# Moving one step of a polynomial exp from VectorE to GpSimd in an attention kernel, with a new order of cells and casts

The kernel runs on one core of a Trainium2 chip. The metric is device time in microseconds (us): the median of the runs of one kernel, each run being the time of the core from launch to finish. The kernel before takes 397.42 us (397.2 to 397.73). The device time is about 1.8 us above the span that the profile shows, from the first to the last instruction.

## The reference

Grouped-query attention: 8 batches, 8 query heads that share 2 K/V heads, sequence 1024, head size 64, float32 in and out.

```python
q: (8, 8, 1024, 64)   k, v: (8, 2, 1024, 64)          # times 0.1
for g in range(n_kv_heads):                            # 4 query heads per K/V head
    scores = scale * np.matmul(q_group, k_group.transpose(0, 1, 3, 2))
    attn = np.exp(scores - scores.max(axis=-1, keepdims=True))
    attn = attn / (attn.sum(axis=-1, keepdims=True) + 1e-08)
    output[:, group] = np.matmul(attn, v_group)
```

## The kernel before

The work is cut into 128 **jobs** (batch, head, one of two sets of 512 queries), each of 8 **cells** (128 keys by 512 queries). TensorE makes the scores of a cell into PSUM. A cell then takes one of two ways. ScalarE takes two cells at a time with its exp function ("A" cells, in the PSUM tiles `aps`). VectorE takes single cells ("D" cells, in `dps`): it empties PSUM into integers that are already the bits of a rough bfloat16 exp, and then improves a group of cells with a curve in four steps, which I call AND, linear step, product and add.

```python
def exps(n, cells):                       # ScalarE, two cells
    nc.scalar.activation(out=pt[:, 0:m], in_=psum.pop(("A", n))[:, 0:m], func=AF.Exp, scale=scale)

def exp_bits(cell, n, g, slot):           # VectorE, one cell: empties PSUM
    nc.vector.tensor_scalar(out=groups[g][:, slot], in0=psum.pop(cell),
        scalar1=bits_scale, scalar2=bits_bias, op0=ALU.mult, op1=ALU.add)

def exp_curve(g, m, step):                # a group of GROUP = 4 cells
    if step == 0:    nc.vector.tensor_scalar(out=z, in0=pd, scalar1=0x7F, scalar2=None,
                                             op0=ALU.bitwise_and)          # AND
    elif step == 1:  nc.vector.tensor_scalar(out=y, in0=temps[g][0], scalar1=CURVE_A / 128.0,
                         scalar2=CURVE_B, op0=ALU.mult, op1=ALU.add)       # linear step
    elif step == 2:  nc.vector.tensor_tensor(out=y, in0=z, in1=y, op=ALU.mult)     # product
    else:            nc.vector.tensor_tensor(out=pd, in0=pd, in1=y, op=ALU.add)    # add
```

TensorE multiplies every finished cell with V (plus a column of ones for the sum), and VectorE normalises a job with a reciprocal and a multiplication.

K and q reach their transposed form through DRAM. GpSimd issues a **cast** (float32 to bfloat16 into scratch `scr_q`, `scr_k`, `scr_v`); once scores have begun, each cast also waits for the last score before it in the plan, which paces the casts. SyncE issues two **transposes** for each (`qT`, `kT`), and GpSimd issues four **placements** of `kT` into `kset`.

```python
def cast(key, src):           # GpSimd
    dma = nc.gpsimd.dma_start(out=scr..., in_=src...)
def transpose(key, dst, n):   # SyncE
    nc.sync.dma_start_transpose(out=dst[:, rows], in_=src[rows, :])
def place_k(b, g, side, parity):   # GpSimd
    nc.gpsimd.dma_start(out=ksets[b % 2][...], in_=kT[(b, g)][...])
```

Who does what when is fixed at build time. A small simulation (`make_plan`) gives each operation a planned time from fixed costs. Loads are hung in at planned distances before the first use of what they bring (`th`), and everything is issued in the order of these times. Each engine then works its own queue from front to back.

```python
for op in plan:
    at(op[0], run[op[1]], *op[2:])
...
    at(th - 28.0, cast, ("q", b, h), q[b, h])
    at(th - 17.0 + n, transpose_q, b, h, n)
    ...
    at(th - 27.0 + n, transpose_k, b, g, n)
    at(th - 20.0, place_k, b, g, side, parity)
```

The softmax here doesn't subtract the row's maximum and nothing guards it: scores larger than these inputs give would overflow.

Of the kernel before, what the change touches and what calls it, by code (L numbers as in the profile page):

```python
# [13 lines left out]

GROUP = 4


def make_plan(nj, nkc):
# [5 lines left out]

    QK, PV, EXP, P1, NORM = 0.214, 0.143, 0.925, 0.605, 0.57
    CHAIN = (0.73, 0.73, 1.26, 1.26)
    FROM_PE, FROM_ACT, FROM_DVE = 0.28, 0.18, 0.12
    LIVE_A, LIVE_D, PENDING, ONLY_A = 26, 6, 8, 14
    INF = 1e9
    n = nj * nkc  # L30
    ops = []
    pe = act = dve = 0.0
    a_free, bank, obank_free = [0.0, 0.0], [0.0, 0.0], [0.0, 0.0]
    nxt = 0
    open_jobs, next_job, rem, obank = [], 0, {}, {}
    open_a = None
# [4 lines left out]
    a_id = d_id = -1  # L41

    def first_free(slots):
        return min(range(len(slots)), key=lambda s: slots[s])

    while normed < nj:
        best = None
        if nxt < n:
            ta = td = INF
            if open_a is not None:  # L50
                ta = max(pe, open_a["t"])
            elif live["A"] < LIVE_A:
                ta = max(pe, min(a_free))
            if pending < PENDING and nxt < n - ONLY_A and (cur or live["D"] < LIVE_D):
                td = max(pe, min(bank))
            t, to_d = (ta, 0) if ta <= td else (td, 1)
            if t < INF:
                best = min(best or (INF,), (t, 1 + to_d, "qk", to_d))
        for i, s in enumerate(open_jobs):
            for c in rem[s]:  # L60
                at = max(pe, ready.get(s * nkc + c, INF))
                if at < INF:
                    best = min(best or (INF,), (at, 3 + i, "pv", (s, c)))
        if len(open_jobs) < 2 and next_job < nj:
            at = max(pe, min(obank_free), min(ready.get(next_job * nkc + c, INF) for c in range(nkc)))
            if at < INF:
                best = min(best or (INF,), (at, 3 + len(open_jobs), "open", next_job))
        for q, p, kind in ((normq, 0, "norm"), (p1q, 1, "p1"), (chainq, 2, "chain")):
            if q:
                best = min(best or (INF,), (max(dve, q[0][0]), p, kind, 0))  # L70
        if cur and nxt >= n - ONLY_A and not p1q:
            best = min(best or (INF,), (dve, 9, "flush", 0))
        t, _, kind, arg = best
        if kind == "qk":
            cell = nxt
            nxt += 1
            pe = t + QK
            if not arg:
                if open_a is None:
                    slot = first_free(a_free)  # L80
                    a_id += 1
                    live["A"] += 1
                    open_a = {"slot": slot, "t": a_free[slot], "cells": []}
                    a_free[slot] = INF
                o = open_a
                ops.append((t, "qk", cell, "A", a_id, o["slot"], len(o["cells"])))
                o["cells"].append(cell)
                home[cell] = ("A", a_id)
                if len(o["cells"]) == 2 or nxt >= n:
                    act = max(act, pe + FROM_PE)  # L90
                    ops.append((act, "exp", a_id, tuple(o["cells"])))
                    act += EXP * len(o["cells"]) / 2
                    a_free[o["slot"]] = act + FROM_ACT
                    uses[("A", a_id)] = len(o["cells"])
                    for x in o["cells"]:
                        ready[x] = act + FROM_ACT
                    open_a = None
            else:
                k = first_free(bank)
                bank[k] = INF  # L100
                pending += 1
                ops.append((t, "qk", cell, "D", k, 0, 0))
                p1q.append((pe + FROM_PE, cell, k))
# [44 lines left out]
        else:  # L148
            _, g, cells, step = chainq.pop(0)
            ops.append((t, "chain", g, len(cells), step))  # L150
            dve = t + CHAIN[step] * len(cells) / GROUP
            if step + 1 < len(CHAIN):
                chainq.insert(0, (dve, g, cells, step + 1))
            else:
                pending -= len(cells)
                uses[("D", g)] = len(cells)
                for x in cells:
                    ready[x] = dve + FROM_DVE
# [4 lines left out]
def kernel(  # L163
# [7 lines left out]
    nc = tc.nc  # L171
# [18 lines left out]
    E1 = D + 1  # L190
    PIECE = 256
    scale = 1.0 / math.sqrt(D)
    bits_scale = 128.0 * scale * math.log2(math.e)
# [13 lines left out]
    first_pool = ctx.enter_context(tc.tile_pool(name="firstp", bufs=1))  # L207
    qT_pool = ctx.enter_context(tc.tile_pool(name="qTpool", bufs=8))
    kT_pool = ctx.enter_context(tc.tile_pool(name="kTpool", bufs=4))
    pa_pool = ctx.enter_context(tc.tile_pool(name="papool", bufs=26))  # L210
    pd_pool = ctx.enter_context(tc.tile_pool(name="pdpool", bufs=6))
    tmp_pool = ctx.enter_context(tc.tile_pool(name="tmppool", bufs=2))
# [67 lines left out]
    def place_v(b, g):  # L280
        for two in range(2):
# [5 lines left out]
            )  # L287

    def first_loads():

        staged = []
        for eng, src in ((nc.sync, k[0, 0]), (nc.scalar, q[0, 0])):
            f = first_pool.tile([128, NHC, 2, D], FP32, name=f"f{len(staged)}")
            eng.dma_start(
                out=f, in_=src.rearrange("(c p two) d -> p c two d", p=128, two=2)
            )
            staged.append(f)
        vf = first_pool.tile([128, NHC, 2, D], FP32, name="vf")
        nc.sync.dma_start(
            out=vf, in_=v[0, 0].rearrange("(c p two) d -> p c two d", p=128, two=2)  # L300
        )
        cast(("q", 0, 1), q[0, 1])
        for two in range(2):
# [3 lines left out]
            )  # L307
        for side in range(2):
            nc.gpsimd.memset(ksets[1][(1 - side) * D : (2 - side) * D, :, side, :], 0.0)  # L309
        fk, fq = staged  # L310

        hk = first_pool.tile([128, NHC, 3, D], BF16, name="hk")
        nc.vector.tensor_copy(out=hk[:, :, 0:2, :], in_=fk)  # L313
        nc.vector.tensor_copy(out=hk[:, :, 2, :], in_=fk[:, :, 0, :])
        hq = first_pool.tile([128, NHC, 2 * D], BF16, name="hq")
        nc.scalar.copy(out=hq, in_=fq.rearrange("p c two d -> p c (two d)"))
        tk = dbanks[0].tile([128, 2, HALF], BF16, name="dps0")
        tq = dbanks[1].tile([128, HALF], BF16, name="dps1")
        for w in range(2):
            for c in range(NHC):  # L320
                nc.tensor.transpose(  # L321
# [3 lines left out]
                )  # L325
        for c in range(NHC):
            nc.tensor.transpose(tq[:, c * 128 : (c + 1) * 128], hq[:, c, :], ident)
        qT[(0, 0)] = qT_pool.tile([128, HALF], BF16, name="qT")
        lo, hi = slice(0, D), slice(D, 2 * D)
        nc.vector.tensor_copy(out=ksets[0][lo, 0, 0, 0:HALF], in_=tk[lo, 0, :])  # L330
        nc.scalar.copy(out=qT[(0, 0)], in_=tq)
        nc.vector.tensor_copy(out=ksets[0][lo, 0, 0, HALF:S], in_=tk[lo, 1, :])
        nc.vector.tensor_copy(out=ksets[0][hi, 0, 1, 0:HALF], in_=tk[hi, 1, :])
        nc.vector.tensor_copy(out=ksets[0][hi, 0, 1, HALF:S], in_=tk[hi, 0, :])

# [45 lines left out]
    def exp_curve(g, m, step):  # L381
# [7 lines left out]
        elif step == 1:  # L389
            y = tmp_pool.tile([128, GROUP, QBS], FP16, name="y")[:, 0:m]  # L390
            temps[g].append(y)
            nc.vector.tensor_scalar(  # L392
                out=y,
# [55 lines left out]
    for op in plan:  # L449
        if op[1] == "qk":  # L450
            first_use.setdefault(op[2] // NKC, op[0])
        at(op[0], run[op[1]], *op[2:])
    for b in range(B):
        for h in range(H):
            if b == 0 and h == 0:
                continue
            th = first_use[(b * H + h) * 2]
            if (b, h) != (0, 1):
                at(th - 28.0, cast, ("q", b, h), q[b, h])
            for n in range(HALF // PIECE):  # L460
                at(th - 17.0 + n, transpose_q, b, h, n)
            if h % HPG == 0:
                g = h // HPG
                at(th - 38.0, cast, ("k", b, g), k[b, g])
                at(th - 33.0, cast, ("v", b, g), v[b, g])
                for n in range(HALF // PIECE):
                    at(th - 27.0 + n, transpose_k, b, g, n)
                for side in range(2):
                    for parity in range(2):
                        at(th - 20.0, place_k, b, g, side, parity)  # L470
                at(th - 15.0, place_v, b, g)
# [34 lines left out]
```

## Time and profile before

The span is 395.6 us. Times in a timeline are counted from the start of the span. The prediction divides the span into what precedes the first exp, the exps, and what follows the last; it shows the busy table, the costliest groups and the timelines.

The view of the transfers in the first 16 us gives a queue with its packets, megabytes and share of the 16 DMA engines, and a group of issues with the median us from issue to landing (the last figure).

```profile
q0 software_dynamic: 192, 0.84, 31.9%
...
qT<-scr_q SPq DMA_TRANSPOSE x4, 3.1
```

In the head of the kernel before, ScalarE is busy for 11.46 of 11.80 us, the DMA engines are half used, and the transposes of q land 3.1 us after their issue. The software queue is the one with GpSimd's casts.

### The profile page before, as it was taken

Reading aid. Unit: us, or ns where it says so; the run is one execution under the profiler, and the core shown is the slowest. Engines: PE = TensorE matmul, PEld = TensorE weight load, DVE = VectorE, ACT = ScalarE, POOL = GpSimd, SP = SyncE. Lnnn points to the kernel's source line nnn. Section 1 sums busy time; section 2 is a strip of 40 time slices with the busy share of each in tenths; the row PEclk is TensorE's granted clock in tenths of the full one; section 3 lists DMA queues with packets and bytes.
Section 4 is the critical chain, followed back from the end, with each engine's and each line's share of the span. In section 5 each row is a group of like instructions: output and inputs, shape, how many; then the busy total and the mean of one; then the engine's idle time right before and its main releaser. Section 6 shows DMA issues by size and latency. Waiting matters only on the chain.

```text
span 395.6 us, 12683 instructions
## 1 busy us (share of the span) xinstructions
PE 365.7 (92%) x5043; PEld 233.0 (59%) x5132; DVE 375.8 (95%) x664; ACT 381.5 (96%) x415; POOL 86.6 (22%) x165
## 2 busy tenths in 40 slices
PE   4899999999999999999999999999999999999986
PEld 2455566565656556655656565565655666565655
DVE  4999999999999999999999999999999999999995
ACT  4999999999999999999999999999999999999992
POOL 5340303132041313113131040312214131120000
PEclk9999999999999999999999999999999999999999
DMA  4665866749676786847758686785965867574314
GB/s 106 106 125 111 163 107 127 128 86 160 103 139 130 132 143 101 142 90 145 115 103 141 111 141 112 118 143 98 155 109 115 149 132 121 99 130 99 68 28 94
DMA packets 134890, 46.72 MB, mean 118 GB/s; under 512 B 130848, under 2 KB 132384, under 8 KB 133344
## 3 DMA queue, kind: packets, MB, share of 16 engines
q1 hardware_dynamic: 129408, 29.52, 38.3%
q0 software_dynamic: 4896, 16.13, 27.0%
q8 instruction: 40, 0.66, 0.8%
q10 hardware_dynamic: 528, 0.26, 0.2%
q14 instruction: 18, 0.15, 0.2%
HBM read 27.13 MB, written 28.97 MB: 142 GB/s over the span
## 4 chain that ended last, share of the span: by engine, by line
ACT 67%; DVE 11%; PE 10%; issue 6%; DMA 3%; POOL 1%; SPq 0%
ACT pa L362 67%; PE ops L414 5%; PE aps L351 5%; DVE pd L371 3%; DVE y L402 2%; DVE pd L406 2%; DVE ost L429 1%; DMA vf<-in_v_dram 1%; PE dps L351 1%; DVE y L392 1%; DMA qT<-scr_q 1%; POOL kset L309 1%; DVE z L386 1%; DVE rec L427 1%; DMA scr_q<-in_q_dram 1%
## 5 line engine op out<-in xcount | busy, mean ns | idle before, releaser
L362 ACT ACTIVATE pa<-aps 128x1024 bf16<-128x1024 f32 x412 | 379.0, 1064 | 2.1 <-PE aps L351 1.3
L351 PE MATMUL aps<-qT,kset 128*128 128x512 bf16 x735 | 226.2, 379 | 15.5 <-ACT pa L362 13.6
L414 PEld LDWEIGHTS <-pa 128*128 128x128 bf16 x3296 | 134.5, 97 | 57.6 <-DVE ost L429 0.8
L414 PE MATMUL ops<-vset,pa 128*128 128x65 bf16 x3296 | 143.9, 193 | 3.4
L371 DVE TENSOR_SCALAR pd<-dps 128x512 uint16<-128x512 f32 x200 | 129.8, 682 | 2.2 <-PE dps L351 2.2
L351 PEld LDWEIGHTS <-kset 128*128 128x128 bf16 x1024 | 85.3, 97 | 66.3 <-issue 30.9
L248 POOL DMA_DIRECT2D scr_q<-in_q_dram x63 | 34.0, 540 | 173.4 <-PE aps L351 150.6
L351 PE MATMUL dps<-qT,kset 128*128 128x512 bf16 x200 | 64.5, 380 | 1.0
L406 DVE TENSOR_TENSOR pd<-pd,y 128x2048 uint16<-128x2048 uint16 x50 | 61.2, 1225 | 1.7
L402 DVE TENSOR_TENSOR y<-z,y 128x2048 f16<-128x2048 uint16 x50 | 61.2, 1225 | 1.7
L429 DVE TENSOR_TENSOR ost<-ops,rec 128x256 f32<-128x256 f32 x128 | 54.3, 425 | 4.4
L414 PEld LDWEIGHTS <-pd 128*128 128x128 bf16 x800 | 38.5, 97 | 29.8 <-DVE pd L406 7.9
L268 POOL DMA_DIRECT2D kset<-kT x60 | 32.2, 545 | 76.7 <-DMA kT<-scr_k 68.7
L414 PE MATMUL ops<-vset,pd 128*128 128x65 bf16 x800 | 45.3, 194 | 1.2
L392 DVE TENSOR_SCALAR y<-z 128x2048 f16<-128x2048 uint16 x50 | 34.3, 687 | 0.6
L386 DVE TENSOR_SCALAR z<-pd 128x2048 uint16<-128x2048 uint16 x50 | 34.2, 684 | 0.0
L427 DVE RECIPROCAL rec<-ops 128x4 f32<-128x4 f32 x128 | 22.6, 176 | 2.4 <-PE ops L414 1.9
L248 POOL DMA_DIRECT2D scr_v<-in_v_dram x15 | 7.6, 505 | 8.2 <-PE aps L351 7.1
L248 POOL DMA_DIRECT2D scr_k<-in_k_dram x15 | 8.1, 542 | 4.7 <-PE aps L351 4.3
L321 PE MATMUL dps<-ident,hk 128*128 128x128 bf16 x8 | 1.0, 311 | 5.0 <-DVE hk L313 5.0
L321 PEld LDWEIGHTS <-hk 128*128 128x128 bf16 x8 | 0.8, 141 | 5.0 <-DVE hk L313 5.0
L309 POOL MEMSET kset<- 64x2048 bf16 x2 | 3.6, 1798 | 0.1
(20 smaller groups left out, 9.7 us busy)
## 6 DMA issues: line engine op xcount, KB each, us to landing
out_dram<-ost SPq DMA_DIRECT2D x128, 128.0 KB, 3.2
scr_q<-in_q_dram POOLq DMA_DIRECT2D x63, 128.0 KB, 3.5
kset<-kT POOLq DMA_DIRECT2D x60, 64.0 KB, 2.7
qT<-scr_q SPq DMA_TRANSPOSE x126, 3.6
scr_k<-in_k_dram POOLq DMA_DIRECT2D x15, 128.0 KB, 4.2
scr_v<-in_v_dram POOLq DMA_DIRECT2D x15, 128.0 KB, 3.9
vset<-scr_v SPq DMA_DIRECT2D x30, 64.0 KB, 3.8
kT<-scr_k SPq DMA_TRANSPOSE x30, 3.4
```

The lines of the kernel that those rows point to most:

```text
L248: dma = nc.gpsimd.dma_start(out=scr.rearrange("(p f) -> p f", f=1024), in_=src.rearrange("(p s) d -> p (s d)", s=1024 // D),)
L268: nc.gpsimd.dma_start(out=ksets[b % 2][side * D : (side + 1) * D, g, side, parity * HALF : (parity + 1) * HALF], in_=kT[(b, g)][parity * D ...
L351: last_score[0] = nc.tensor.matmul(dst, lhsT=ksets[b % 2][:, h // HPG, side, c * 128 : (c + 1) * 128], rhs=qT[(b, h)], start=True, stop=Tr ...
L362: nc.scalar.activation(out=pt[:, 0:m], in_=psum.pop(("A", n))[:, 0:m], func=AF.Exp, scale=scale)
L371: nc.vector.tensor_scalar(out=groups[g][:, slot], in0=psum.pop(cell), scalar1=bits_scale, scalar2=bits_bias, op0=ALU.mult, op1=ALU.add,)
L386: nc.vector.tensor_scalar(out=z, in0=pd, scalar1=0x7F, scalar2=None, op0=ALU.bitwise_and)
L392: nc.vector.tensor_scalar(out=y, in0=temps[g][0], scalar1=CURVE_A / 128.0, scalar2=CURVE_B, op0=ALU.mult, op1=ALU.add,)
L402: nc.vector.tensor_tensor(out=y, in0=z, in1=y, op=ALU.mult)
L406: nc.vector.tensor_tensor(out=pd, in0=pd, in1=y, op=ALU.add)
L414: nc.tensor.matmul(ops_of[s][:, qs, :], lhsT=p_of[cell][:, qs * 128 : (qs + 1) * 128], rhs=vsets[b % 2][:, h // HPG, c, :], start=opens an ...
L427: nc.vector.reciprocal(out=rec, in_=o[:, :, D])
L429: nc.vector.tensor_tensor(out=ost, in0=o[:, :, 0:D], in1=rec.unsqueeze(2).to_broadcast([128, NQS, D]), op=ALU.mult,)
```

## The change

The intent is to relieve VectorE, so that it can take more cells from ScalarE. The linear step goes to GpSimd and runs there while VectorE empties PSUM. Groups grow from 4 to 8 cells. VectorE's cells come from jobs up to six further on (`LEAD`, growing by one every three jobs, `RAMP`), so that little is left at the end. Because those jobs come earlier, and because the planned distances before first use grow (for q in the first batch from 28 to 40), casts are issued sooner. The first loads come in halves, and 28 small matmuls warm TensorE.

```diff
-GROUP = 4
+GROUP = 8
+POOL_STEP = 1
...
+    LIVE_A, LIVE_D, PENDING, PER_JOB, LEAD, RAMP, AHEAD, FIRST_PV = 28, 5, 16, 2, 6, 3, 0.08, 2.0
...
+        lead = min(LEAD, job_a // RAMP)
+        job_d = max(job_d, job_a + lead)
+        while job_d < nj and (taken[job_d] >= PER_JOB or not todo[job_d]):
+            job_d += 1
...
-    qT_pool = ctx.enter_context(tc.tile_pool(name="qTpool", bufs=8))
+    qT_pool = ctx.enter_context(tc.tile_pool(name="qTpool", bufs=10))
...
-            nc.vector.tensor_scalar(
+            nc.gpsimd.tensor_scalar(
                 out=y,
                 in0=temps[g][0],
...
+    for side in range(2):
+        at(20.0 + 3.0 * side, blank_k, side)        # two memsets of the second K set, on GpSimd
...
-                at(th - 28.0, cast, ("q", b, h), q[b, h])
+                at(th - (34.0 if b else 40.0), cast, ("q", b, h), q[b, h])
-                at(th - 17.0 + n, transpose_q, b, h, n)
+                at(th - (21.0 if b else 17.0) + n, transpose_q, b, h, n)
...
-                at(th - 38.0, cast, ("k", b, g), k[b, g])
-                at(th - 33.0, cast, ("v", b, g), v[b, g])
+                at(th - 46.0, cast, ("k", b, g), k[b, g])
+                at(th - 42.0, cast, ("v", b, g), v[b, g])
-                    at(th - 27.0 + n, transpose_k, b, g, n)
+                    at(th - (31.0 if b else 19.0) + n, transpose_k, b, g, n)
-                        at(th - 20.0, place_k, b, g, side, parity)
+                        at(th - (15.0 if b else 8.0), place_k, b, g, side, parity)
```

Cut: the rest of the plan's new costs, the sizes of two other pools (`pa` 26 to 28, `pd` 6 to 5), and the first loads in halves.

## The prediction

> **What bounds the kernel now.** I read the page first: its busy table and its costliest groups.
>
> ```profile
> PE 365.7 (92%) x5043; PEld 233.0 (59%) x5132; DVE 375.8 (95%) x664; ACT 381.5 (96%) x415; POOL 86.6 (22%) x165
> L362 ACT ACTIVATE pa<-aps 128x1024 bf16<-128x1024 f32 x412 | 379.0, 1064 | 2.1 <-PE aps L351 1.3
> L371 DVE TENSOR_SCALAR pd<-dps 128x512 uint16<-128x512 f32 x200 | 129.8, 682 | 2.2 <-PE dps L351 2.2
> L406 DVE TENSOR_TENSOR pd<-pd,y 128x2048 uint16<-128x2048 uint16 x50 | 61.2, 1225 | 1.7
> L402 DVE TENSOR_TENSOR y<-z,y 128x2048 f16<-128x2048 uint16 x50 | 61.2, 1225 | 1.7
> L392 DVE TENSOR_SCALAR y<-z 128x2048 f16<-128x2048 uint16 x50 | 34.3, 687 | 0.6
> L386 DVE TENSOR_SCALAR z<-pd 128x2048 uint16<-128x2048 uint16 x50 | 34.2, 684 | 0.0
> ```
>
> ScalarE makes 412 exps of two cells each in 379.0 us, so 0.920 us apiece, and waits only 2.1 us before them. It is the bound. VectorE, which makes the other 200 of the 1024 cells, is as full: the two share the cells in proportion to speed. So the span has three parts: what precedes the first exp, the exps, and what follows the last. The timeline of ScalarE gives the first and third edges.
>
> ```profile
> 6.48 0.58 ACT L331 COPY qT<-dps 128x512 bf16<-128x512 bf16 x1 [0.93 <-PE dps L327]
> 8.16 6.04 ACT L362 ACTIVATE pa<-aps 128x1024 bf16<-128x1024 f32 x6 [1.10 <-PE aps L351]
> ...
> 384.37 3.84 ACT L362 ACTIVATE pa<-aps 128x1024 bf16<-128x1024 f32 x4
> ```
>
> First exp at 8.16, last one done at 388.21: 380.05 us between. The other 395.6 - 388.21 = 7.4 us are a tail in which TensorE works off products (the chain of waits ends in 3.14 us of them), VectorE normalises and the last output lands. The device time, 397.4, is 1.8 above the span.
>
> Last I read GpSimd's timeline and SyncE's, because the change puts arithmetic into GpSimd's queue, which until now holds almost only transfers.
>
> ```profile
> 10.37 0.52 POOL L248 DMA_DIRECT2D scr_q<-in_q_dram  x1
> ...
> 22.12 2.29 POOL L268 DMA_DIRECT2D kset<-kT  x4 [8.64 <-DMA kT<-scr_k]
> 24.40 0.52 POOL L248 DMA_DIRECT2D scr_q<-in_q_dram  x1
> ```
> ```profile
> 6.17 9.48 SPq L260 DMA_TRANSPOSE qT<-scr_q  x4
> 15.69 2.99 SPq L260 DMA_TRANSPOSE kT<-scr_k  x2
> ```
>
> GpSimd stands still for 8.64 us before it can issue the four placements of the second K group, since the transposes that make kT are issued by SyncE at 15.69 and land at 22.1. The cast behind them waits too, although it needs none of it: the queue is in order. Today this costs nothing. The reader should keep it in mind.
>
> **What the Trainium skill says.** "VectorE: DVE Perf Modes", section "The perf-mode tier table (the rule you actually need)", gives 693 ns for a 2048-element 16-bit tensor_scalar and 1224 ns for tensor_tensor. The trace agrees (684 to 687, and 1225). "SBUF — State Buffer", section "Who interferes with whom", says that a Vector instruction in a 2-port mode, or with two SBUF inputs against a GpSimd read, excludes GpSimd from a shared port, while one with at most one SBUF input outside those modes doesn't. No GpSimd arithmetic runs beside VectorE in the steady part of this trace, so nothing here tests it. "GPSIMD Engine Reference", section "4.1 Engine selection", calls one-input elementwise work on GpSimd roughly line-rate; section "3.1 Elementwise — side-by-side cycle accounting" has 1.03 cycles per element for light bodies. The trace's nearest rows are GpSimd's memset, 1798 ns for 2048 elements (0.88 ns each), and its casts, two of 256 elements in 0.74 us; both fit.
>
> **The change part by part.** Counts are from the instruction order of both builds.
> 1. Cells. ScalarE gets 406 exps instead of 412: 6 x 0.920 = 5.5 us less. The exps then need 406 x 0.920 = 373.5 us.
> 2. VectorE. The linear step leaves it, and groups have 8 cells. 212 emptyings at a pitch of 0.60 (two take 1.28 in the timeline) = 127; 128 normalisations at 0.55 = 70; 26 ANDs of 4096, estimated 684 + 2048/4/0.96 = 1217 ns, = 32; 52 tensor_tensors, estimated 1225 + 2048/2/0.96 = 2292 ns, = 119; one group of four adds 3. Sum 351 instead of about 391 at the same pitches (120 + 70 + 50 x 4.0). So VectorE gets some 30 us of slack, but the longest thing that holds it grows from 1.2 to 2.3 us.
> 3. GpSimd. 26 linear steps of 4096. Estimate from the memset's rate: 4096 x 0.88 + 0.2 = 3.8 us; with the skill's 1.03 cycles, 3.7. In every group the order puts only emptyings and normalisations of VectorE between the AND and the product: mostly 3 or 4 with 2 normalisations (about 3.5 us) or 6 with 3 (about 5.3 us). They read PSUM, so by the skill they aren't locked out, and the step is about hidden. Leftover waits: 1 us, a guess.
> 4. Head. K and q come in halves, TensorE is warmed by 28 small matmuls. The second half lands about when the whole did; TensorE saves 0.43 of the first two score matmuls' 0.86, but the warm-up itself may last till 5.5 to 6.0 (28 x 0.11 to 0.13 from 2.4) and hold up the transposes. I take the first exp at 7.5, 0.7 sooner.
> 5. Tail. VectorE's cells lie six jobs ahead, so at the end few products are left: two cells behind the last exp (0.2 + 0.3), then normalisation 0.9 and 3.1 us as now from the last ost to the end: 4.5 instead of 7.4, 2.9 less.
> 6. Casts sooner. Two memsets leave GpSimd's queue (3.65 us), and the casts start at about 7.1 instead of 10.37.
>
> Without a new wait: 7.5 + 373.5 + 1 + 4.5 = 386.5, plus 1.8 = 388.3. That would be 2.3% faster.
>
> **The new wait.** In the new order GpSimd's queue has the four kset placements of the second K group right in front of the first linear step. In SyncE's queue the transposes come as q1, q2, q3 (two each), then K's two. A transpose takes SyncE about 1.2 us. With q2's cast landing near 10 and q3's near 12.4, K's go out at 15 to 17 and land 4 to 4.6 later: at about 20.8. Four issues of 0.55 follow, so the first linear step starts at S = 23.1 and ends at 26.9. Its AND is done near 14.5.
> VectorE's queue has six emptyings after the AND and then the product that needs that step; the next two emptyings stand behind it. TensorE's queue has, behind the two D scores of those two emptyings, three more pairs for ScalarE, then D scores that need their banks. So the D score can't start before S + 3.85 + 2.3 + 0.6 + 0.1, and the second one, the next pair and the exp follow at S + 8.25 = 31.4. ScalarE has by then 18 exps: 7.5 + 18 x 0.92 = 24.1, with 0.7 more for q1's transpose, which lands at 11.3 where the order wants it near 10.5. It is then starved for about 31.4 - 24.8 = 6.6 us, and since it's the bound the loss is final. With K landing 2 us sooner or later the loss is 4.6 or 8.6.
> Sum: 386.5 + 0.7 + 6.6 = 393.8, plus 1.8 = 395.6. I lean a little to the lower side, as DMA times in the head are the shakiest of these: **394.8 us**, 0.7% faster.
>
> **The rivals.**
> A: the change works as it is meant to, K's transposes land early enough or fewer cells hang on the first group. Time 388 to 390. For it: every transfer starts earlier; the part after the head is sound. Against it: the in-order queue, shown by the 8.64 us wait above, and the position of the linear step behind it.
> B: the linear step on GpSimd is slow, or is held by port exclusion or transfers in its queue, in every group. Each us beyond about 3.8 stalls VectorE in some half of 27 groups, then TensorE's D scores. At 6 us per step: about 14 x 2.2 + 12 x 0.7 = 39 us less a part hidden in ScalarE's one exp of stock, so 405 to 430. Against it: memset and cast rates in this trace, and no Vector instruction with a second SBUF input inside the interval.
> C: nothing is stalled in the head, but 2.3 us tensor_tensors block both PSUM banks and starve ScalarE a little in each group, 26 x 0.2 = 5 us: 393. Against it: VectorE has slack, and D scores stand where the order expects a free bank.
>
> **Range and chances.** Main line 392 to 397 with about 70%, A 13%, C with or on top of the main line some 10%, B 7%. That gives 390 to 398.5 for 8 in 10. Two per cent faster means under 389.5: only A does it, 0.13. Two per cent slower is over 405.4: B, 0.06. Same: 0.81.
>
> **What would show it.** Right: ScalarE's exps 406 at about 0.92 mean pitch; a gap of 4 to 9 us in them between 23 and 33 us, with y's first instruction on GpSimd starting right behind four kset issues near 23 and the first product on VectorE waiting for POOL; hardly any gap after 40 us; first exp near 7.5; last exp to end near 4.5; GpSimd's linear step near 3.8 us; VectorE busy some 340 to 355 us. Wrong: kT landing before 16 us, or ScalarE without a gap in the head (A); a linear step over 5 us, or many waits of VectorE on POOL all along (B); many short waits of ScalarE all along with no long one (C).

## More of the kernel before

A line of the busy times by stretch gives start and end of the stretch, its length, busy time and number of instructions of TensorE, its weight loads, VectorE, ScalarE and GpSimd, the granted TensorE clock, the DMA share and GB/s.

```profile
8.20:20.00 11.80, 10.43 (x90) 5.14 (x91) 10.25 (x16) 11.46 (x13) 5.23 (x8) 1.00 0.57 96
```

## The result, and the profile after

The changed kernel takes **402.07 us** (four runs: 400.8, 401.2, 402.95, 403.05). The ratio to the kernel before is 1.0115, with a 95% interval of 1.0078 to 1.0151. Ratios here are the mean time of one kernel's fast runs over that of the other's in the same rounds, so they are not quite the ratio of the medians that are quoted. Executions over 1.5% slower than the fastest of the same kernel are left out of the means. The kernel became slower by about 1.2%, where 0.7% faster was predicted, and it lies above the predicted range. All kernels gave correct results.

First the page of the changed kernel, its busy table and costliest groups.

```profile
PE 368.8 (92%) x5160; PEld 232.6 (58%) x5160; DVE 352.7 (88%) x558; ACT 378.0 (95%) x410; POOL 182.1 (46%) x192
L407 ACT ACTIVATE pa<-aps 128x1024 bf16<-128x1024 f32 x406 | 375.3, 1053 | 12.4 <-PE aps L396 11.5
L416 DVE TENSOR_SCALAR pd<-dps 128x512 uint16<-128x512 f32 x212 | 137.7, 683 | 15.2 <-PE dps L396 14.1
L437 POOL TENSOR_SCALAR y<-z 128x4096 f16<-128x4096 uint16 (+1 forms) x27 | 95.6, 3542 | 79.2 <-DVE rec L472 53.1
L447 DVE TENSOR_TENSOR y<-z,y 128x4096 f16<-128x4096 uint16 (+1 forms) x27 | 60.7, 2248 | 10.8 <-POOL y L437 10.6
```

The intended effect is there. VectorE has fallen from 375.8 to 352.7 us, it takes 212 cells, and the step on GpSimd takes 3.54 us in the mean (3.60 for a full group). But ScalarE, the bound, now waits 12.4 us before its exps; it had waited 2.1. Its timeline (start, length, instructions, and in brackets the wait in front) says where.

```profile
7.82 8.59 ACT L407 ACTIVATE pa<-aps 128x1024 bf16<-128x1024 f32 x9 [0.68 <-PE aps L396]
22.84 1.02 ACT L407 ACTIVATE pa<-aps 128x1024 bf16<-128x1024 f32 x1 [6.43 <-PE aps L396]
24.03 7.44 ACT L407 ACTIVATE pa<-aps 128x1024 bf16<-128x1024 f32 x8 [0.16 <-PE aps L396]
33.56 1.94 ACT L407 ACTIVATE pa<-aps 128x1024 bf16<-128x1024 f32 x2 [2.09 <-PE aps L396]
...
43.40 2.01 ACT L407 ACTIVATE pa<-aps 128x1024 bf16<-128x1024 f32 x2 [1.20 <-PE aps L396]
...
379.82 15.05 ACT L407 ACTIVATE pa<-aps 128x1024 bf16<-128x1024 f32 x16
```

The reader sees a wait of 6.43 us after only nine exps, then two smaller ones of 2.09 and 1.20. With two of 0.16 and 0.18 they make 10.06 us, all before 45 us. What TensorE waited for in the first one stands in its own timeline:

```profile
14.63 0.59 PE L396 MATMUL aps<-qT,kset 128*128 128x512 bf16 x2
20.92 1.03 PE L396 MATMUL dps<-qT,kset 128*128 128x512 bf16 x2 [5.69 <-DMA qT<-scr_q]
```

It needed the transposed q of the third head (q2; heads count from 0) for a D score, and stood still for 5.69 us. The views of the first 16 us of transfers and of the stretches show why q2 was late.

```profile
q0 software_dynamic: 322, 1.39, 51.2%
...
qT<-scr_q SPq DMA_TRANSPOSE x6, 8.3
```
```profile
8.20:20.00 11.80, 6.60 (x71) 3.56 (x70) 6.63 (x10) 8.13 (x9) 5.19 (x11) 1.00 1.02 169
20.00:24.00 4.00, 3.08 (x8) 1.13 (x9) 1.98 (x3) 1.02 (x1) 0.60 (x2) 0.57 0.64 99
```

Thirteen casts go out between 7.08 and 14.6 us, q2's the first of them. The casts' queue moves 1.39 MB instead of 0.84, the DMA share between 8.2 and 20 us is 1.02 instead of 0.57, and q's transposes land 8.3 us after their issue in the median instead of 3.1 (q2's first one after 10.2). This agrees with the Trainium skill, "DMA: Bandwidth & Descriptors", section "Issuing engines are not separate DMA queues": transfers of whatever engine run on the same 16 DMA engines and interleave. The second stretch also shows the granted TensorE clock at 0.57 after the stop. The skill's "TensorE: Matmul & The Clock Gate", "Part 1: The HAM clock gate", says that after one idle window of about 3.4 us the clock falls to half, and the trace agrees.

Last, GpSimd's timeline where its first linear step stands, and VectorE's wait for it:

```profile
23.40 2.08 POOL L294 DMA_DIRECT2D kset<-kT  x4 [8.78 <-DMA kT<-scr_k]
25.51 3.63 POOL L437 TENSOR_SCALAR y<-z 128x4096 f16<-128x4096 uint16 x1
```
```profile
29.17 2.29 DVE L447 TENSOR_TENSOR y<-z,y 128x4096 f16<-128x4096 uint16 x1 [2.99 <-POOL y L437]
```

The budget of both profiled runs (the changed kernel's is its fastest, 400.8 us):

| us | before | after |
|---|---|---|
| first exp starts | 8.16 | 7.82 |
| exps | 412 | 406 |
| exps at the pitch of before's mid-run, 0.9206 | 379.3 | 373.8 |
| waits of ScalarE before 45 us (listed above) | | 10.06 |
| rest between first and last exp | 0.75 | 3.2 |
| last exp to the end | 7.4 | 4.1 |
| span | 395.6 | 399.0 |

The pitch is the mean distance from start to start of two exps, taken from the hundredth exp to shortly before the end; it is 0.9206 before and 0.9269 after. So the change earned 5.5 us of exps, 3.3 us of tail and 0.3 of head, and gave back 10.1 us in the first 45 us and 2.5 in small waits. The other runs of the changed kernel take 0.4 to 2.25 us more than the profiled one, at a clock of 0.984 to 0.987 against 0.996.

### The profile page after: what moved, and what is told of

The parts are those of the page before. It is cut to its first block, busy times and chain, and to the rows that moved or that the text cites. A ratio compares the mean times of both kernels' runs of the same rounds, so it can differ in the third digit from the quotient of the medians.

```text
span 399.0 us, 12714 instructions
## 1 busy us (share of the span) xinstructions
PE 368.8 (92%) x5160; PEld 232.6 (58%) x5160; DVE 352.7 (88%) x558; ACT 378.0 (95%) x410; POOL 182.1 (46%) x192
## 4 chain that ended last, share of the span: by engine, by line
ACT 66%; PE 10%; DVE 9%; issue 6%; POOL 4%; DMA 4%; SPq 0%; POOLq 0%; ACTq 0%
ACT pa L407 66%; PE aps L396 5%; PE ops L459 4%; DVE pd L451 3%; POOL y L437 3%; DVE pd L416 2%; DVE y L447 2%; DMA kT<-scr_k 1%; DMA scr_v<-in_v_dram 1%; PE dps L396 1%; DMA vf<-in_v_dram 1%; DVE z L431 1%; DVE ost L474 1%; POOL scr_q L274 1%; POOL kset L294 0%
## 5 line engine op out<-in xcount | busy, mean ns | idle before, releaser
L407 ACT ACTIVATE pa<-aps 128x1024 bf16<-128x1024 f32 x406 | 375.3, 1053 | 12.4 <-PE aps L396 11.5
L396 PE MATMUL aps<-qT,kset 128*128 128x512 bf16 x812 | 241.7, 379 | 11.7 <-ACT pa L407 10.5
L416 DVE TENSOR_SCALAR pd<-dps 128x512 uint16<-128x512 f32 x212 | 137.7, 683 | 15.2 <-PE dps L396 14.1
L437 POOL TENSOR_SCALAR y<-z 128x4096 f16<-128x4096 uint16 (+1 forms) x27 | 95.6, 3542 | 79.2 <-DVE rec L472 53.1
L396 PEld LDWEIGHTS <-kset 128*128 128x128 bf16 x1024 | 81.7, 98 | 70.8 <-issue 31.5
L396 PE MATMUL dps<-qT,kset 128*128 128x512 bf16 x212 | 74.5, 382 | 9.6 <-DMA qT<-scr_q 5.7
L447 DVE TENSOR_TENSOR y<-z,y 128x4096 f16<-128x4096 uint16 (+1 forms) x27 | 60.7, 2248 | 10.8 <-POOL y L437 10.6
L451 DVE TENSOR_TENSOR pd<-pd,y 128x4096 uint16<-128x4096 uint16 (+1 forms) x27 | 60.6, 2243 | 0.1
L431 DVE TENSOR_SCALAR z<-pd 128x4096 uint16<-128x4096 uint16 (+1 forms) x27 | 34.1, 1262 | 0.0
L274 POOL DMA_DIRECT2D scr_v<-in_v_dram x15 | 7.5, 501 | 15.6 <-PE dps L396 8.8
L340 PE MATMUL ops<-ident 128*128 128x128 bf16 x28 | 3.2, 313 | 2.5 <-POOL ident masks.py:199 2.5
(19 smaller groups left out, 12.4 us busy)
```

Of the source, the lines that this page charges most:

```text
L274: dma = nc.gpsimd.dma_start(out=scr.rearrange("(p f) -> p f", f=1024), in_=src.rearrange("(p s) d -> p (s d)", s=1024 // D),)
L396: last_score[0] = nc.tensor.matmul(dst, lhsT=ksets[b % 2][:, h // HPG, side, c * 128 : (c + 1) * 128], rhs=qT[(b, h)], start=True, stop=Tr ...
L437: nc.gpsimd.tensor_scalar(out=y, in0=temps[g][0], scalar1=CURVE_A / 128.0, scalar2=CURVE_B, op0=ALU.mult, op1=ALU.add,)
```

## The experiments

My theory after the comparison: the casts issued sooner crowd the DMA engines, so that q2 and then K arrive late; that costs the 6.4 us, and behind it the linear step, which stands behind the placements in GpSimd's queue, costs the rest. The rivals: the linear step's place in the queue is the whole loss, and the casts are incidental; or the linear step on GpSimd is itself what costs; or the cells taken from later jobs do, by asking for q2 too soon.

### The first two linear steps on VectorE

```diff
-            nc.gpsimd.tensor_scalar(
+            (nc.vector if g < 2 else nc.gpsimd).tensor_scalar(
```

> Changed kernel, but the linear step of the first two groups is made on VectorE (so it doesn't stand in GpSimd's queue behind the K placements). Theory (two separate head losses: a flood of casts holds back the transposes of q2, and the first linear step stands behind the placements): the gap of 6.4 us before ScalarE's tenth exp stays, the gaps of 2.1 and 1.2 us after it go to under 0.5, the time falls by 2 to 3.5 us to about 399. Rival (GpSimd's step is what slows the kernel, in every group): 25 of 27 groups still have it, so the time moves by less than 0.5 us.

Measured: 401.71 us over all four runs, ratio of the fast ones 1.0078 (1.0035 to 1.0122). The profile fell in the one run (408.19 us) that counts as slow; the fast ones are 399.33, 400.51 and 402.9, with a median of 400.51. The gain over the changed kernel is not resolved, as the intervals overlap. So the two first linear steps are not the main loss. The slow run's profile keeps a first wait of 7.5 us, as it should if q2 is late. It also shows, late in the run, what one late `kT` can do (the chain that ended last, in order of time: start, length, what):

```profile
196.87 4.08 DMA kT<-scr_k
201.55 1.40 POOL kset L294 x3
203.65 3.64 POOL y L437
207.31 2.30 DVE y L447
```

A late transpose holds the placements, these hold the linear step, that holds VectorE's product. It is the predicted wait, in mid-run, in one run; it says nothing of the medians.

### Casts spread out

```diff
-                at(th - (34.0 if b else 40.0), cast, ("q", b, h), q[b, h])
+                at(th - ((27.0 if b == 1 else 34.0) if b else 20.0), cast, ("q", b, h), q[b, h])
-                at(th - (21.0 if b else 17.0) + n, transpose_q, b, h, n)
+                at(th - (21.0 if b else (14.0 if h > 1 else 17.0)) + n, transpose_q, b, h, n)
-                at(th - 46.0, cast, ("k", b, g), k[b, g])
-                at(th - 42.0, cast, ("v", b, g), v[b, g])
+                first = (b, g) in ((0, 1), (1, 0))
+                at(th - ((31.0 if b else 25.0) if first else 46.0), cast, ("k", b, g), k[b, g])
+                at(th - ((21.0 if b else 15.0) if first else 42.0), cast, ("v", b, g), v[b, g])
... (kT of the next batch and the copy of v later in the same way)
```

> Changed kernel, but of the first batch only four casts are issued before the first scores (now ten or so), the rest is paced by later scores. Theory: the transposes of q2 land in 3 to 5 us instead of 10 and the gap of 6.4 us shrinks under 1.5 us; the linear step of the first group, which still stands behind the K placements, then becomes the wait, with a gap of 4 to 6.5 us near 25 us; time 397 to 400.5. Rival (transposes in the head are slow whatever is issued): the 6.4 us gap stays. Rival (only one loss): the time falls by the whole 6 us to about 395.5.

Measured: 400.31 us, ratio 1.0061 (1.0046 to 1.0076). The median landing of q's transposes in the first 16 us falls from 8.3 to 5.9 us, and the first wait falls with it:

```profile
20.26 1.02 ACT L407 ACTIVATE pa<-aps 128x1024 bf16<-128x1024 f32 x1 [3.69 <-PE aps L396]
```

It goes from 6.43 to 3.69 us and not to under 1.5, so the crowding is a part of q2's delay and not all of it. The waits behind the linear step stay (1.34 us in place of 2.09, and 1.35 later).

### Both of these

The edit is the two above together.

> Both edits of the two runs before it. Theory: no gap in ScalarE's exps over 1.5 us; span about 7.8 + 406 x 0.92 + 3 + 4.1 + 1.5 = 390, time 391 to 393.5, so 1 to 1.6 per cent under the kernel before. Rival (steady state of the changed kernel is slower than that of the one before): time stays above 395.

Measured: 398.11 us over all four runs, one of them slow; the fast ones have a median of 397.49 and a ratio of 1.0000 (0.9976 to 1.0024). It is the first to get back to the kernel before, but it misses what I expected by at least 4.0 us: waits of 2.53, 0.71, 0.62 and 1.69 us remain. The expectation took the losses as two, each removed whole; neither edit removed its one whole.

### All linear steps on VectorE

```diff
-            nc.gpsimd.tensor_scalar(
+            nc.vector.tensor_scalar(
```

> Changed kernel, but the linear step of all groups on VectorE, same order. Theory: the head gap behind the placements goes (-3 us), but VectorE's load rises by 26 x 1.26 = 33 us to about 386 of 395, so it has hardly slack left and starves ScalarE in places: time 398 to 406. Rival (GpSimd's step, port exclusion or its waits are what cost time): under 397.

Measured: 409.62 us, ratio 1.0299 (1.028 to 1.0318), more than I expected. The busy table:

```profile
PE 365.1 (90%) x5068; PEld 233.2 (57%) x5160; DVE 379.9 (93%) x585; ACT 379.7 (93%) x410; POOL 90.9 (22%) x165
```

With the same plan, VectorE is back at 379.9 us and the pitch of the exps rises to 0.952. So moving the step to GpSimd is worth 409.62 - 402.07 = 7.6 us in this plan. The rival that blames the step itself falls.

### Casts spread, and the placements behind a linear step

```diff
-        at(20.0 + 3.0 * side, blank_k, side)
+        at(12.0 + 2.0 * side, blank_k, side)
+    lines = [op[0] for op in plan if op[1] == "chain" and op[4] == POOL_STEP]
+    def behind_line(t, latest):
+        later = [x for x in lines if x >= t - 2.0]
+        if later and later[0] <= latest:
+            return later[0] + 0.001
+        return max(x for x in lines if x <= t) + 0.001
...
-                        at(th - (15.0 if b else 8.0), place_k, b, g, side, parity)
+                        at(behind_line(th - (15.0 if b else 8.0), th - 7.0), place_k, b, g, side, parity)
```

> As e2 (casts of the first batch spread), and in addition every set of four K placements is put into GpSimd's queue behind a linear step instead of in front of one (the two memsets also earlier). Theory (in the queue in order, a late kT holds the linear step, that the product on VectorE, that TensorE's scores): the first linear step starts as soon as its AND is done, ScalarE's gap near 30 us and the later ones over 1 us go, time 396 to 398 against 400.3 of e2; and since a late kT can no longer stall the core in mid-run, no run lies over 1.5 us above the fastest. Rival (the scatter of the changed kernel comes from the clock alone): the scatter of 2 to 6 us stays.

Measured: 395.07 us, ratio 0.9943 (0.9924 to 0.9961), 0.9 us under the range that I expected, and faster than the kernel before. The runs spread over 1.54 us (1.5 expected, against 2.25 in the changed kernel). GpSimd's timeline and ScalarE's:

```profile
16.02 3.62 POOL L437 TENSOR_SCALAR y<-z 128x4096 f16<-128x4096 uint16 x1
21.28 2.18 POOL L294 DMA_DIRECT2D kset<-kT  x4 [1.64 <-DMA kT<-scr_k]
```
```profile
20.03 22.13 ACT L407 ACTIVATE pa<-aps 128x1024 bf16<-128x1024 f32 x24 [3.43 <-PE aps L396]
```

The linear step now runs at 16.02 instead of 25.51, and the placements still wait for `kT`, but nobody waits behind them. ScalarE then works 24 exps without a stop. What remains is the wait for q2, 3.43 us.

### A slower start of the lead

On top of the last one: `RAMP` 3 to 6, so that VectorE's cells move ahead by one job every six jobs, and q2 is needed later.

> As e5, but VectorE's cells run ahead by one more job per six jobs of ScalarE instead of per three, so that q2 is first needed some 4 us later. Theory (what is left in the head is TensorE waiting in order for the transposes of q2): gap before ScalarE's tenth exp under 0.7 us, time 1.5 to 3 us under e5, 393.5 to 395.5. Rival (the head is bound by transfers in any case and the gap only moves): same as e5 within 1 us.

Measured: 398.67 us, ratio 1.0019 (0.9989 to 1.0049), a miss. The first wait does shrink, to 1.75 us. But this run doesn't show that the lead's demand made q2 late: the casts hang on the first use, so a slower ramp moves them too, and the DMA share between 8.2 and 20 us falls from 1.02 to 0.68. And the load distances were set for the old ramp, and TensorE now waits in mid-run. The waits between 100 and 300 us (engine and what it makes, what it waited for: us in total, times, longest):

```profile
PE dps L396 <- DMA qT<-scr_q: 6.1, 5, 1.8
```

The pitch of the exps rises to 0.948, which costs more than the head earned.

### No lead

On top of the same one: `LEAD` 6 to 0.

> As e5, but VectorE's cells come from the job at hand or the next one, as in the kernel before. Theory (the lead hides the longer chain of a group of eight and GpSimd's step, and empties the tail): TensorE's products wait for VectorE's cells, the tail after the last exp is 7 us or more instead of 4.1, time 400 to 412. Rival (the lead brings nothing but the early need for q): time under e5.

Measured: 421.16 us, ratio 1.0588 (1.056 to 1.0617), in the expected direction and far beyond the expected size. The last exp ends at 399.65 of a span of 420.3, so the tail is 20.6 us, and the pitch is 0.976. The plan also splits the cells otherwise (399 exps, 226 cells on VectorE), so the size isn't the lead's alone. The lead earns more than its head costs; it should be kept and fed.

### q2's cast early

On top of the spread and the placements behind: q2's cast right behind q1's, ahead of the two copies of v, which wait for a load (4.0 us in the changed kernel).

```diff
         cast(("q", 0, 1), q[0, 1])
+        cast(("q", 0, 2), q[0, 2])
...
-            if (b, h) != (0, 1):
+            if (b, h) not in ((0, 1), (0, 2)):
```

> As e5, but the cast of q2 is issued right behind that of q1, before GpSimd's two copies of v, which wait for v's load. Theory: q2 is there when TensorE wants it, gap under 0.7 us, time 393.5 to 395.5. If the early cast delays the loads of K and q instead, the first exp comes later than 8.2 us and the gain is eaten.

Measured: 392.34 us, ratio 0.9859 (0.9833 to 0.9886), a little better than expected.

```profile
20.64 39.77 ACT L408 ACTIVATE pa<-aps 128x1024 bf16<-128x1024 f32 x43 [1.34 <-PE aps L397]
```

The wait of 3.43 us is gone; a wait of 1.34 us for q3 is left, and then 43 exps run without a stop.

### Only q2's cast early

The same edit in the changed kernel, without the others.

> Changed kernel with one edit: the cast of q2 is issued right behind that of q1, the other casts flood as before. Theory (what counts is that q2's transposes are issued before the flood): q2's transposes are issued near 8 us, the gap of 6.4 us shrinks to under 2 us, but q3 and kT then come out of the flood late and the first linear step still stands behind the placements (gap 3 to 6 us near 25 us): time 397 to 401. If the flood alone is to blame (the transposes wait in the DMA engines however early they are issued), the gap stays over 4 us and the time at 401 to 403.

Measured: 402.36 us, ratio 1.0117 (1.0093 to 1.0141): nothing gained. The time is that of the second expectation, but its reason isn't: q2's transposes, issued at 8.18 and 9.47 us, landed at 13.1 and 16.6, before most of the crowd.

```profile
24.86 1.94 ACT L408 ACTIVATE pa<-aps 128x1024 bf16<-128x1024 f32 x2 [4.28 <-PE aps L397]
...
35.19 1.94 ACT L408 ACTIVATE pa<-aps 128x1024 bf16<-128x1024 f32 x2 [3.64 <-PE aps L397]
```

While the transfers are crowded, the wait moves to q3 (4.28 us), and the one behind the linear step, no longer hidden by the first, grows from 2.09 to 3.64.

### Only the placements behind a linear step

The edit of the placements (with the memsets, which it moves too) in the changed kernel, without spread casts.

> Changed kernel with one edit: each set of K placements stands behind a linear step in GpSimd's queue, memsets earlier; casts as in the changed kernel. Theory: the 6.4 us gap stays, the 2.1 and 1.2 us gaps after it go; time 397.5 to 400, no run with a stall in mid-run. Rival (the first gap hides the second, so nothing is gained alone): 401 to 403.

Measured: 397.33 us, ratio 0.9998 (0.9975 to 1.0021), so 402.07 - 397.33 = 4.7 us less than the changed kernel.

```profile
23.86 1.02 ACT L407 ACTIVATE pa<-aps 128x1024 bf16<-128x1024 f32 x1 [7.20 <-PE aps L396]
...
27.95 32.44 ACT L407 ACTIVATE pa<-aps 128x1024 bf16<-128x1024 f32 x35 [0.50 <-PE aps L396]
```

The waits of 2.09 and 1.20 are gone, that for q2 stays at 7.20. The two losses have different causes. Of the 4.7 us between the medians the two profiles show only 2.3 (spans 399.0 and 396.7), since one is the fastest run of its kernel and the other the slowest; where the rest lies is not shown.

### q3 before K

On top of the kernel with q2 early: K's first transposes one unit later in the plan, so that q3's second one stands before them in SyncE's queue.

```diff
-    at(th - ((25.0 if first else 31.0) if b else 19.0) + n, transpose_k, b, g, n)
+    at(th - ((25.0 if first else 31.0) if b else 18.0) + n, transpose_k, b, g, n)
```

> e8 and the second transpose of q3 before the first of K in SyncE's queue. Theory: the last gap of the head (1.3 us, TensorE waiting for q3) shrinks to 0.3 us or less; time 0.5 to 1.2 us under e8, so about 391.3. It may come back as a later K placement: then same as e8.

Measured: **391.28 us**, ratio 0.9836 (0.981 to 0.9863), 1.6% under the kernel before and 2.7% under the changed one. Its interval overlaps that of the kernel with q2 early on top of the other two edits, so the step from 392.34 is not resolved, but the wait for q3 is gone:

```profile
16.75 22.13 ACT L408 ACTIVATE pa<-aps 128x1024 bf16<-128x1024 f32 x24 [0.39 <-PE aps L397]
39.87 145.16 ACT L408 ACTIVATE pa<-aps 128x1024 bf16<-128x1024 f32 x157 [0.99 <-PE aps L397]
```

The longest wait between the exps is now 0.99 us. The first exp starts at 7.30, the last ends at 385.22, the tail is 4.1 and the span 389.3. It beats both kernels.

### More buffers for the transposed q

On top of that: `qT_pool` with 16 buffers instead of 10.

> e11 and 16 buffers instead of 10 for the transposed q. Theory (in mid-run SyncE's transposes wait for a free buffer, which makes q and kT late for cells that run six jobs ahead; TensorE waited 4.5 us for one near 123 us in e8): these waits go, mean pitch of the exps in mid-run from 0.930 to 0.925 or less, time 1 to 2 us under e11, 389 to 390.5. Rival (the mid-run losses come from the 2.3 us instructions of VectorE): same as e11 within 0.4 us.

Measured: 391.61 us, ratio 0.9853 (0.9835 to 0.9871). Nothing changes, and the pitch is 0.9271 (0.9267 without). The buffers of `qT` do not make the small waits of mid-run.

### Groups of four

On top of the version with q3 before K: `GROUP` 8 to 4, with twice the buffers for groups, so that the products take 1.22 us instead of 2.25.

> The kernel of the run before the last (casts spread, placements behind the linear step, q2 early, q3 before K) with groups of four cells instead of eight, as the kernel before had them, and twice the buffers for them, so the longest VectorE instruction falls from 2.29 to 1.23 us and the linear step on GpSimd from 3.6 to about 1.85 us. If the 2.3 us products cause the small waits of ScalarE in mid-run (mean pitch of exps 0.927 against 0.9206 in the kernel before), the pitch falls to 0.922 or less and the time from 391.3 to 389 to 390. If they come from elsewhere (order of scores, waits for GpSimd), the pitch stays at 0.926 to 0.930 and the time at 391 to 393; the fixed costs of 27 more groups on VectorE (about 0.06 x 4 x 26 = 6 us) find room in its slack.

Measured: 415.93 us, ratio 1.0462 (1.0448 to 1.0475). Both expectations missed, for a reason that neither had: the plan finds room for only 180 cells on VectorE, so ScalarE gets 422 exps. Its groups:

```profile
L408 ACT ACTIVATE pa<-aps 128x1024 bf16<-128x1024 f32 x422 | 389.2, 1062 | 8.2 <-PE aps L397 7.2
...
L448 DVE TENSOR_TENSOR y<-z,y 128x2048 f16<-128x2048 uint16 x45 | 55.0, 1223 | 57.2 <-POOL y L438 57.1
```

VectorE waits 57.1 us for GpSimd, against 5.8 with groups of eight. The reason for larger groups shows here: the steps on GpSimd need enough other work of VectorE to hide behind. On the small waits it speaks only weakly, since there are fewer D cells: the pitch is 0.9258, so shorter products did not bring it back to 0.9206. Distances over 0.97 us fell from 33 to 14 in mid-run, but the median distance rose from 0.912 to 0.9175.

### Only the memsets early

The changed kernel with only the memsets moved from 20 and 23 to 12 and 14 in the plan, to separate them from the placements.

> The changed kernel with only the two memsets of the second K set moved from 20 and 23 to 12 and 14 in the plan's time; the placements stay where they are. If the 4.7 us gained by moving placements and memsets together come from the placements, this run stays at 401 to 403 and the linear step still starts at 25 or later; if the memsets had a share, it comes to 398 to 400.5, or, as they now stand ahead of the placements with 3.6 us of work, it could lose: linear step later than 26.5 and 402 to 405.

Measured: 400.53 us, ratio 1.0086 (1.0068 to 1.0104). The interval overlaps that of the changed kernel (1.0078 to 1.0151), and the median is at the very edge of what the rival expected. In the profile the first wait (6.33 us) and the linear step's start (25.29) stay, while the wait of 1.20 us after 43 us is gone. By the medians the memsets had some 1.5 of the 4.7 us and the placements the other 3 or so. The first share is not resolved, the second is: the intervals of this run and of the one with the placements moved (0.9975 to 1.0021) lie apart.

## Why the prediction was right and wrong

**The bound and what the exps cost: right.** ScalarE stayed the bound, made 406 exps, and the pitch was 0.927 for the 0.920 assumed. VectorE was busy for 352.7 us (351 in the sum, 340 to 355 as the sign), the linear step took 3.60 us for a full group (3.7 to 3.8), the AND 1.22 in the median and the product 2.29. (Two slips of the prediction change nothing: 120 + 70 + 50 x 4.0 is 390, not 391, and in the kernel before K's transposes had landed at 21.84; 22.1 is when the placements were issued. And the divisors 4, 2 and 0.96 in its part 2 were not read from this trace, though the two times that they gave came out.) The rival that expected a slow or locked-out step falls by the test with all linear steps on VectorE. That the emptyings go on beside it undisturbed also holds: 683 ns in the mean, with 682 before.

**Head and tail: right to some tenths.** First exp 7.82 (7.5), tail 4.1 (4.5).

**The new wait: the mechanism right, its place in the sum wrong.** The linear step did start right behind four placements, at 25.51 instead of 23.1, and the exp that hangs on it started at 33.56, which is 8.05 later (8.25 predicted). But this cost only 2.09 us by then, because ScalarE had lost 6.43 already. The losses overlap: with q2 early alone the second one grew to 3.64, and with only the placements moved the first stayed at 7.20. Moving the placements, with the memsets, is worth 4.7 us by the medians; 6.6 were predicted for the placements alone.

**A wait that the prediction didn't have: the memsets.** The wait of 1.20 us at 43.40 isn't the linear step's. GpSimd's and VectorE's timelines:

```profile
36.93 3.65 POOL L316 MEMSET kset<- 64x2048 bf16 x2
```
```profile
38.87 2.80 DVE L431 TENSOR_SCALAR z<-pd 128x4096 uint16<-128x4096 uint16 x1
```

The second AND started just after the second memset (38.79 to 40.59) and took 2.80 us instead of 1.22. The emptying behind it was late, and TensorE waited 1.29 us for that before its next D score. With q2 early alone an AND beside a memset took 2.53 us. With the memsets early, alone or with the placements, no AND took over 1.28, and this wait is gone. It fits the exclusion of VectorE and GpSimd from a shared port that the prediction took from the skill and could not test in its trace, though no run isolates the port. Part 6 has the memsets leave GpSimd's queue, as a gain; they move to 36.93, and it did not ask what they meet there.

**The step that failed.** It is in "The new wait": "With q2's cast landing near 10 and q3's near 12.4, K's go out at 15 to 17 and land 4 to 4.6 later", together with part 6, "Casts sooner", which booked the earlier casts as free. The times of issue were right: q2's two transposes went out at 10.16 and 11.31, so its cast had landed near 10, and K's at 15.6 and 16.85. The landings were not. By SyncE's transposes one by one, q2's landed 10.2 and 9.6 us after their issue, near 20.4 and 20.9, q3's after 8.8 and 7.8, and K's second after 5.9, while the twelve casts behind q2's went through the same DMA engines. I had given q1 0.7 us and q2 nothing; q2 cost 6.43. My landing times were read from the kernel before, where the DMA engines were half used in this stretch (0.57). I had seen that the change moves casts into just this stretch, and did not ask what they collide with.

That this is the cause, and not only what stands beside it, the experiments show by steps: spreading the casts took the wait from 6.43 to 3.69. Casting q2 early on top of that removed the wait for q2 and left 1.34 for q3. Turning these two transposes in the queue removed that too. No one of these does it alone: with q2 early in the crowd, q3 was late instead. The slower ramp also cut the wait, to 1.75, but it spread the casts as well, so the part of the lead is not separated. Nor did the DMA engines have to be emptied for it: in the best version the DMA share between 8.2 and 20 us is still 0.93, but q2's transposes land at 13.3 and 15.6 us, because q2's cast goes out at 2.37 us, ahead of all but q1's.

**How the miss of 7.3 us adds up** (402.07 against 394.8), by the budget of the profiled run: waits in the head 10.06 instead of 7.3, so 2.8; the rest between first and last exp 3.2 instead of the 1 guessed for leftover waits, so 2.2; the pitch's rounding 0.3; first exp and tail together 0.1 less; the 0.8 by which I had shaded the sum down; and the median above the profiled run, 1.3. That is 7.3. So with these head waits in it the sum would have been 395.6 + 2.8 = 398.4; the small waits were booked too low, and I had no term for runs slower than the profiled one.

**What stays open.** The small waits of mid-run (pitch 0.9267 to 0.9271 in eight of the fourteen versions with groups of eight, the changed kernel among them, against 0.9206) make about 300 x 0.0063 = 2 us. Many and short, they look like the third rival. The buffers of `qT` are ruled out, and shorter products were tested only together with fewer cells. But the traces, read matmul by matmul, show where much of it lies. Between the last A score of one exp and that of the next, TensorE also makes D scores and products with V. In the changed kernel 33 distances of mid-run are over 0.97 us. They include all 12 in which TensorE had two D scores and four product matmuls to make, and all 5 with one D score and twelve. TensorE works these off without a stop, so without a wait for VectorE, in 0.98 to 1.01 us, and together the 17 lie 1.4 us above the pitch of 0.9206. The best version has the same counts. That points to the order in which the plan gives TensorE its work; no run tests another order. The other long distances (15 with sixteen product matmuls, a mix that 121 shorter ones have too, and one with two D scores) stay unexplained, and the trace of the kernel before misses too many matmul records for the same count. It is not shown either why two of the other three runs of the changed kernel are over 2 us longer than the profiled one; they have a lower mean clock, and the best version, without the stop of TensorE, still spreads from 389.66 to 392.0.

## What to carry to other kernels

When a change issues transfers sooner, take the landing times of the kernel before as a lower bound only: count what else will be in the DMA engines in that stretch, and ask which transfer is needed first. Put arithmetic into an engine's queue ahead of transfers whose source may be late, not behind them. Where work on one engine can hold another's (here an AND beside a memset), look at what stands side by side after the change. And expect two waits in the same stretch to hide each other, so that removing one alone may gain nothing.

## What the Trainium skill lacked or had wrong

- "DMA: Bandwidth & Descriptors", "Issuing engines are not separate DMA queues", says that transfers interleave, but gives no measure of how late a small transfer becomes behind queued casts. Here the median landing of q's transposes went from 3.1 to 8.3 us, and the longest of any transfer of `scr_q` from 4.8 to 10.2, when the casts' queue moved 1.39 MB in those 16 us instead of 0.84.
- "GPSIMD Engine Reference" does not say what it means for arithmetic that GpSimd's one queue is worked off in order and also issues transfers, and no other page was found to say it: a linear step of 3.60 us stands behind placements whose source is late (8.78 us of wait). Moving them behind it, with the memsets, was worth 4.7 us.
- "GPSIMD Engine Reference", section "4.1 Engine selection", calls one-input elementwise work roughly line-rate on GpSimd. Read as "as fast as VectorE", this fails here: a 16-bit step of 4096 elements took 3.60 us there, and one on VectorE (the AND, same size) 1.22, so it is 3.0 times slower in this form. The 1.03 cycles per element of section "3.1 Elementwise — side-by-side cycle accounting" did predict it well (3.7 was estimated).
